# An MLP up projection by seven block products, with the sums of its weights built in device memory

## The chip, the cores and the metric

One core of a Trainium2 chip. The metric is the device time of one execution in microseconds; the time before is the median of 3 runs, 828.88 us (828.78 to 829.03). Engines: TensorE (PE, with its weight loads as PEld), VectorE (DVE), ScalarE (ACT), GpSimd (POOL), SyncE (SP, which here only issues DMAs).

## The reference

A transformer-like encoder layer on 512 tokens of width 1024, in float32: a recurrent mixer, cross-attention to 256 memory tokens, a squared-ReLU MLP with 4096 hidden units, a final norm. What the change touches is the last step of the layer:

```python
def squared_relu_mlp(xn, w_up, w_down):
    return jnp.square(jax.nn.relu(xn @ w_up)) @ w_down
...
x = x + squared_relu_mlp(rmsnorm(x, norm_mlp[l]), w_up[l], w_down[l])
return rmsnorm(x, norm_final)
```

`rmsnorm` divides each token's row by its root mean square and multiplies by a gain per column.

## The kernel before

**Precision.** Every float32 product is made of three reduced-precision ones. An operand is split into a high part (a ScalarE copy) and the remainder (a VectorE subtraction); `split_out` (L258) does both. `mm3` (L261 to L263) then issues high x high, high x remainder, remainder x high into one sum in PSUM. The program's order on TensorE is that of the code from the output projection on (`manual_schedule`); on the other engines a scheduler decides it, helped by `high_priority` and by orderings written by hand (`behind`).

**Weights.** They lie in device memory as blocks of 128x1024 (512 KB) in the order in which they are used. `load` (L236) brings a block into one of three staging buffers (`st`) through SP's queue; `split` makes its two parts in one of three pairs (`wh`, `wl`). `weights` splits two blocks ahead and loads one more.

**Seven products.** A product of 2x2 blocks can be made with seven block products in place of eight, when sums of blocks of both operands are used. The output projection of the attention (`by_blocks(-1)`) and the down projection (`by_blocks(f)`) work so: seven products P1 to P7, each in two column groups, makes 14 jobs of 12 matmuls of 512 wide. The sums of weight blocks come from `sum_loads` and `add_block` (L1086 to L1102): GpSimd issues DMAs that load a block into SBUF and accumulate others on top. Products go into PSUM banks and are added into the residual x by VectorE (L1222 in the output projection, L1285 in the MLP).

**The MLP before.** After the output projection, `turn_two` (L1236 to L1243) transposes x into `x3T`, four transposes to a bank, with the gain applied and the two parts made straight from PSUM. The root mean square is not applied to x: `rms_row` (L1264 to L1268) puts its reciprocal (`r4`, a power on GpSimd, L1261) into a row over tokens, and the evacuation of the up product multiplies by it: `max(product, 0) * rrow` on VectorE (L1342), then a square on ScalarE (L1343). The hidden units are done in four passes f of 1024. In each, the up projection is made directly: eight weight blocks of 24 matmuls, each 512 tokens wide. Sums and differences of the hidden activations are made and split (L1350 to L1366), then the down projection follows with seven products. The first up projection starts while the last of x is still being added: `first_two` (L1305 to L1324) uses the finished half of x's columns first.

## Time and profile before

| | |
|---|---|
| median of 3 runs | 828.88 us |
| profiled execution | 828.9 us, its span 826.9 us |
| granted TensorE clock | 0.998 |
| matmuls from the first up product to the last down product | 1440 of 512 wide, starts 491.64 to 819.20 us |
| weight loads by SP | 131 of 512 KB |
| transfers by GpSimd into sums | 76 of 512 KB |

The profile is of one execution. A row of a timeline gives start, duration, engine, line, operation, output and inputs, shape and count, and in brackets the idle time before it and what ended that. A row of grouped lines gives busy time and mean ns of one, then the idle time before. A DMA share is that of the core's 16 DMA engines, averaged.

### The profile page before, as it was taken

The page shows a single profiled execution, that of the slowest core. Times are in us where ns is not written, and L with a number is a line of the kernel's source. Part 1 is how long each engine was busy: PE and PEld are TensorE (multiplying, and loading weights), DVE is VectorE, ACT ScalarE, POOL GpSimd, SP SyncE. Part 2 cuts the span into 40 slices and gives each one's busy share as a digit, 9 for nine tenths or more (in the row PEclk, how much of TensorE's full clock was granted, in tenths as well). Part 3 has the DMA queues.
Part 4 walks back from the last instruction along what each step waited for, and adds up shares of the span by engine and source line. Part 5 has one row for each costly group of instructions (what it writes and reads, how often), then busy time and mean ns, then how long its engine had stood idle before and what let it go on. Part 6 is the DMA issues. An engine that isn't in the chain of part 4 may idle for free.

```text
span 826.9 us, 12625 instructions
## 1 busy us (share of the span) xinstructions
PE 813.4 (98%) x4862; PEld 676.1 (82%) x4862; DVE 590.9 (71%) x1046; ACT 431.9 (52%) x771; POOL 77.7 (9%) x131
## 2 busy tenths in 40 slices
PE   8999999999999999999999999999999999999996
PEld 6788778877878988887888888888888888888885
DVE  6568975699479898545668985676668566756685
ACT  5247564545578485345455675443454345434544
POOL 2000000100010000100100004022102210211001
PEclk9999999999999999999999999999999999999999
DMA  7332223322342334532343349969836982798332
GB/s 277 118 120 91 78 79 106 100 89 79 102 128 78 128 128 154 151 98 83 111 119 76 81 128 302 254 171 275 217 102 182 280 211 91 189 290 207 110 70 101
DMA packets 34125, 118.91 MB, mean 144 GB/s; under 512 B 3921, under 2 KB 4049, under 8 KB 34066
## 3 DMA queue, kind: packets, MB, share of 16 engines
q1 hardware_dynamic: 22832, 77.80, 27.5%
q0 software_dynamic: 10944, 39.85, 21.8%
q8 instruction: 38, 0.62, 0.3%
q10 hardware_dynamic: 290, 0.47, 0.1%
q14 instruction: 21, 0.17, 0.1%
HBM read 116.00 MB, written 2.10 MB: 143 GB/s over the span
## 4 chain that ended last, share of the span: by engine, by line
PE 84%; issue 6%; DVE 6%; ACT 2%; DMA 1%; POOL 1%; POOLq 0%; ACTq 0%; DVEq 0%
PE mm L261 17%; PE mm L263 17%; PE mm L262 17%; PE sm L1153 6%; PE sm L1155 6%; PE sm L1154 6%; PE mm L1153 2%; PE mm L1155 2%; PE mm L1154 2%; DVE wl L258 2%; PE sm L827 1%; PE sm L562 1%; PE sm L486 1%; ACT wh L258 1%; DVE t L759 1%
## 5 line engine op out<-in xcount | busy, mean ns | idle before, releaser
L258 ACT ACTIVATE wh<-st 128x1024 fp32r<-128x1024 f32 x131 | 138.7, 1060 | 185.2 <-PE mm L262 117.9
L261 PE MATMUL mm<-xT,wh 128*128 128x512 f32 x544 | 215.3, 396 | 0.0
L258 DVE TENSOR_TENSOR wl<-st,wh 128x1024 fp32r<-128x1024 f32 x131 | 160.1, 1223 | 76.1 <-ACT wh L258 75.6
L263 PE MATMUL mm<-xT,wl 128*128 128x512 f32 x544 | 212.8, 391 | 0.1
L262 PE MATMUL mm<-xT,wh 128*128 128x512 f32 x544 | 212.4, 390 | 0.3 <-DVE xT L975 0.3
L263 PEld LDWEIGHTS mm<-xT,wl 128*128 128x128 f32 x544 | 102.1, 188 | 21.9 <-DVE wl L258 0.3
L262 PEld LDWEIGHTS mm<-xT,wh 128*128 128x128 f32 x544 | 102.3, 188 | 20.8 <-DVE xT L975 0.9
L261 PEld LDWEIGHTS mm<-xT,wh 128*128 128x128 f32 x544 | 102.2, 188 | 20.7 <-ACT wh L258 0.3
L1102 POOL DMA_DIRECT2D as<-in_wpk x52 | 39.6, 763 | 250.2 <-DVE wl L258 162.0
L1342 DVE SCALAR_TENSOR_TENSOR t<-mm,rg 128x512 f32<-128x512 f32 x32 | 22.0, 691 | 52.1 <-PE mm L263 52.0
L1153 PE MATMUL sm<-wh,yT 128*128 128x512 f32 x128 | 49.8, 389 | 0.0
L1154 PE MATMUL sm<-wl,yT 128*128 128x512 f32 x128 | 49.8, 389 | 0.0
L1155 PE MATMUL sm<-wh,yT 128*128 128x512 f32 x128 | 49.8, 389 | 0.0
L258 ACT ACTIVATE wh<-as 128x1024 fp32r<-128x1024 f32 x26 | 27.6, 1062 | 37.0 <-PE sm L1155 23.7
L258 DVE TENSOR_TENSOR wl<-as,wh 128x1024 fp32r<-128x1024 f32 x26 | 31.9, 1226 | 14.0 <-ACT wh L258 14.0
L1153 PE MATMUL sm<-wh,a 128*128 128x512 f32 x84 | 32.9, 391 | 0.0
L1155 PE MATMUL sm<-wh,a 128*128 128x512 f32 x84 | 32.7, 389 | 0.0
L1154 PE MATMUL sm<-wl,a 128*128 128x512 f32 x84 | 32.7, 389 | 0.0
L1285 DVE TENSOR_TENSOR vv<-vv,sm 128x512 f32<-128x512 f32 x48 | 31.0, 681 | 1.7 <-PE sm L1155 1.7
L199 POOL TENSOR_TENSOR tiny<-tiny,misc 128x4 f32<-128x4 f32 (+1 forms) x10 | 9.6, 963 | 201.3 <-DVE tiny L197 136.2
L1155 PEld LDWEIGHTS sm<-wh,yT 128*128 128x128 f32 x128 | 24.0, 188 | 5.0
L1154 PEld LDWEIGHTS sm<-wl,yT 128*128 128x128 f32 x128 | 24.0, 188 | 5.0
(329 smaller groups left out, 1566.8 us busy)
## 6 DMA issues: line engine op xcount, KB each, us to landing
st<-in_wpk SPq DMA_DIRECT2D x131, 512.0 KB, 3.4
as<-in_wpk POOLq DMA_DIRECT2D x52, 512.0 KB, 6.9
gate<-in_wpk POOLq DMA_DIRECT2D x24, 512.0 KB, 7.1
as<-in_x SPq DMA_DIRECT2D x4, 512.0 KB, 6.8
vv<-in_x SPq DMA_DIRECT2D x8, 256.0 KB, 4.0
out<-vv SPq DMA_DIRECT2D x7, 256.0 KB, 2.2
a<-in_mem SPq DMA_DIRECT2D x2, 512.0 KB, 3.7
t<-in_rows SPq DMA_DIRECT2D x2, 256.0 KB, 5.3
```

The lines of the kernel that those rows point to most:

```text
L199: gp.tensor_tensor(out=r, in0=ms, in1=nh.to_broadcast([P, w]), op=ALU.pow)
L258: return sc.activation(dst_hi, src, AF.Copy), v.tensor_tensor(out=dst_lo, in0=src, in1=dst_hi.bitcast(F32), op=ALU.subtract)
L261: pe.matmul(ps, lhsT=ah, rhs=bh, start=first, stop=False)
L262: pe.matmul(ps, lhsT=ah, rhs=bl, start=False, stop=False)
L263: pe.matmul(ps, lhsT=al, rhs=bh, start=False, stop=last)
L486: mm = pe.matmul(ps[b * i:b * i + b, z:z + b], lhsT=kc[j][:, w * P + b * i:w * P + b * i + b], rhs=rhs(j, w * P, i), start=True, stop=True)
L1102: return gp.dma_start(out=dst, in_=wpk[idx], **kw)
L1153: pe.matmul(ps, lhsT=ah, rhs=bh, start=new, stop=False, **fl)
L1154: pe.matmul(ps, lhsT=ah, rhs=bl, start=False, stop=False, **fl)
L1155: pe.matmul(ps, lhsT=al, rhs=bh, start=False, stop=end and k == 1, **fl)
L1285: added = v.tensor_tensor(out=z, in0=z, in1=ps, op=ALU.add if sign > 0 else ALU.subtract)
L1342: v.scalar_tensor_tensor(out=y, in0=ps, scalar=0.0, in1=rrow[:, 0:512], op0=ALU.max, op1=ALU.mult)
```

## The change

The up projection of each pass is now made by seven block products too (`up`): the tokens are halved into 256 and 256, the 1024 columns of x into two halves, the hidden units into two. A stage has 14 products (P1 to P7, groups a and b of hidden units) of 24 matmuls, 128x256 each. `MORDER` sets the order of products by hand; in all up stages but the first, group a is mostly ahead of group b. Stages are numbered 0 to 7, even ones up, odd ones down.

Sums of weight blocks for the up products P4 to P7, and for P7 of the down product, are built in device memory. `make_forms` yields the steps: a copy of a block into a form (or of one form into another) on SP, and an accumulating DMA on GpSimd. `next_form` issues one step per weight block that an earlier part of the program uses, and on every second product in the MLP. In all there are 40 copies and 40 accumulations, of which 9 and 15 are left when the MLP begins. The finished forms are loaded like plain blocks. The sums for P5, P6, P4 of the down product stay in SBUF, in two buffers (`msum`) filled by `sum_base` on SP and `sum_add` on GpSimd.

As the products are added and subtracted before the ReLU, the root mean square must be applied to x before them. It is done in two halves of tokens: `rstd_half` makes the power of a half, `flip` transposes, ScalarE evacuates with the gain (L1396), `norm_half` transposes the reciprocals, puts them into a row (L1430), multiplies x by it (`times_r`, L1417) and makes and splits the sums of x that the products need (L1439 to L1445). The evacuation of the up product is then ReLU and square on ScalarE, with sums on VectorE around them. Splits per pass rise from 22 to 28.

The diff, cut to its core:

```diff
+    def next_form():
+        o = next(form_steps, None)
+        if o is not None:
+            behind(o, last_load[0] if o.ins.engine == mybir.EngineType.SP else last_made[0])
...
+        if i >= 6 and (i < 46 or i % 3):
+            next_form()
...
+    def mblock(st, g, kh, c):
+        f = st // 2
+        if st % 2:
+            return wpk[SIDX["t", "down", f * 8 + 2 * g + 4 * kh, 512 * c]]
+        i = SIDX["d", "up", 0, 1024 * f + 512 * c + 256 * g]
+        return wpk[i:i + 2, :, kh * 512:kh * 512 + 512].rearrange("n p c -> p n c")
+    def mfill(eng, dst, st, g, b, accumulate=False):
+        kw = dict(accum_op=ALU.add) if accumulate else {}
+        if st % 2 == 0:
+            dst = dst.rearrange("p (n c) -> p n c", n=2)
+        return eng.dma_start(out=dst, in_=mblock(st, g, *b), max_dma_last_dim=4096, **kw)
...
+    def make_forms():
+        def steps(st):
+            f, todo = {}, []
+            for g in range(2):
+                for p in ("P5", "P7", "P6", "P4") if st % 2 == 0 else ("P7",):
+                    f[p, g] = mforms[st, p, g] = hbm.tile([P, 1024], F32, tag=f"f{st}{p}{g}", name=f"form_{st}_{p}_{g}")
+            def start(p, g):
+                return mfill(nc.sync, f[p, g][:, :], st, g, (0, 1))
+            def follow(src, dst, g):
+                return nc.sync.dma_start(out=f[dst, g][:, :], in_=f[src, g][:, :], max_dma_last_dim=4096)
+            def add(p, g, b):
+                formed.add((st, p, g))
+                return mfill(gp, f[p, g][:, :], st, g, b, True)
+            first = ("P7", "P5") if st % 2 == 0 else ("P7",)
+            for p in first:
+                todo += [(start, p, g) for g in range(2)]
+            for p in first:
+                todo += [(add, p, g, (1, 1) if p == "P7" else (0, 0)) for g in range(2)]
+            if st % 2 == 0:
+                for src, dst, b in (("P7", "P6", (0, 0)), ("P6", "P4", (1, 0))):
+                    todo += [(follow, src, dst, g) for g in range(2)] + [(add, dst, g, b) for g in range(2)]
+            return todo
+        for s0 in (0, 4):
+            lanes = [steps(s0), steps(s0 + 1) + steps(s0 + 3), steps(s0 + 2)]
+            while any(lanes):
+                for w in lanes:
+                    if w:
+                        fn, *args = w.pop(0)
+                        yield fn(*args)
+    form_steps = make_forms()
...
+    MORDER = []
+    for q in range(4):
+        MORDER += [seq("1a 2a 1b 6a 5a 7a 3a 4a 5b 6b 2b 7b 3b 4b" if q else "1a 2a 1b 2b 5a 5b 3a 6a 6b 7a 7b 4a 3b 4b"),
+                   two(*("P1", "P5", "P6", "P2", "P7", "P3", "P4") if q < 3 else ("P1", "P5", "P2", "P6", "P3", "P7", "P4"))]
+    MJ = [(st, p, g) for st in range(8) for p, g in MORDER[st]]
...
+    def mload(n):
+        if n < len(MJ) and n not in mst:
+            st, p, g = MJ[n]
+            if st % 2 and p in ("P5", "P6", "P4"):
+                mst[n] = msum[p != "P5"][:, g * 1024:g * 1024 + 1024]
+                return
+            mst[n] = T("st", 1024, 3)
+            if p in PLAIN:
+                last_load[0] = mfill(nc.sync, mst[n][:, :], st, g, PLAIN[p])
+            else:
+                assert (st, p, g) in formed
+                last_load[0] = nc.sync.dma_start(out=mst[n], in_=mforms[st, p, g][:, :], max_dma_last_dim=4096)
...
+    def sum_base(st, p, g):
+        t = msum[p != "P5"][:, g * 1024:g * 1024 + 1024]
+        if p == "P5":
+            mfill(nc.sync, t, st, g, (0, 1))
+        else:
+            assert (st, "P7", g) in formed
+            nc.sync.dma_start(out=t, in_=mforms[st, "P7", g][:, :], max_dma_last_dim=4096)
+    def sum_add(st, p, g):
+        mfill(gp, msum[p != "P5"][:, g * 1024:g * 1024 + 1024], st, g, (1, 0) if p == "P4" else (0, 0), True)
...
+            mload(n)
+            hi, lo = T("wh", 1024, 3, F32R), T("wl", 1024, 3, F32R)
+            last_made[0] = split_out(hi, lo, mst[n])[1]
+            mhl[n] = (hi, lo)
+            if st % 2 and p == "P6":
+                due.append((n + 1, sum_add, st, "P4", g))
+            if st % 2 and p in ("P5", "P4") and st < 7:
+                q = {"P5": "P5", "P4": "P6"}[p]
+                due.append((n + 3, sum_base, st + 2, q, g))
+                due.append((n + 7, sum_add, st + 2, q, g))
+        return mhl[n]
...
+    def mahead(n):
+        with tc.high_priority():
+            for m in range(n, n + 3):
+                msplit(m)
+            for m in range(n + 3, n + 7):
+                mload(m)
+        if n % 2:
+            next_form()
+        return mhl[n]
...
+        with (tc.high_priority() if (t, c) in ((1, 1), (3, 0)) else ExitStack()):
             stats(st2, t, c)
+            if (t, c) in ((1, 1), (3, 0)):
+                rstd_half(t // 2)
+        if (t, c) == (2, 0):
+            turn_x2[0] = [smb(), smb()]
+            later.append([1, lambda: flip(turn_x2[0], (2,), 0)])
+        elif (t, c) == (3, 0):
+            later.append([0, lambda: flip(turn_x2[0], (3,), 0)])
+            later.append([1, lambda: norm_half(1)])
+        elif t % 2:
+            later.append([0 if (t, c) == (1, 1) else 3, lambda: flip([smb(), smb()], (t - 1, t), c)])
+            if (t, c) == (1, 1):
+                later.append([1, lambda: norm_half(0)])
...
+    def flip(banks, ts, c):
+        for i, ps in enumerate(banks):
             for k in range(2):
...
+                for t in ts:
+                    z = k * 256 + (t % 2) * P
+                    pe.transpose(ps[:, z:z + P], xr[t, c][:, (2 * i + k) * P:(2 * i + k) * P + P], ident)
+        t = ts[-1]
+        if t % 2 == 0:
+            return
...
+                sc.activation(fx[t // 2, c][:, kk * 256:kk * 256 + 256], banks[kk // 2][:, (kk % 2) * 256:(kk % 2) * 256 + 256], AF.Copy,
+                              scale=vc[:, V_MLP + 4 * c + kk:V_MLP + 4 * c + kk + 1])
+            if (t, c) == (3, 0):
+                sraw[0] = A4()
+                for h in range(2):
+                    z = slice(h * 512, h * 512 + 512)
+                    v.tensor_tensor(out=sraw[0][:, z], in0=fx[1, 0][:, z], in1=fx[1, 1][:, z], op=ALU.subtract)
...
+    def times_r(x, u, h):
+        z = x[:, h * 512:h * 512 + 512]
+        r = rrow[:, u * 256:u * 256 + 256]
+        v.tensor_tensor(out=z.rearrange("p (k t) -> p k t", t=256), in0=z.rearrange("p (k t) -> p k t", t=256),
+                        in1=r.unsqueeze(1).to_broadcast([P, 2, 256]), op=ALU.mult)
+    def part_split(p, x, h):
+        z = slice(h * 512, h * 512 + 512)
+        split_out(xf[p][0][:, z], xf[p][1][:, z], x[:, z])
+    def norm_half(u):
+        ps = smb()
+        for t in range(2):
+            pe.transpose(ps[:, t * P:t * P + P], rt[u][:, t:t + 1].to_broadcast([P, P]), ident)
+        with tc.high_priority():
+            sc.activation(rrow[:, u * 256:u * 256 + 256], ps[:, 0:256], AF.Copy)
+            for p, x in ((("P1", fx[0, 0]), ("P2", fx[0, 1])) if u == 0 else (("P5", sraw[0]),)):
+                for h in range(2):
+                    times_r(x, u, h)
+                    part_split(p, x, h)
+        if u == 0:
+            return
+        d = sraw[0]
+        x1, x3_, x2_, x4 = fx[0, 0], fx[0, 1], fx[1, 0], fx[1, 1]
+        v.tensor_tensor(out=d, in0=d, in1=x1, op=ALU.subtract)
+        v.tensor_tensor(out=x3_, in0=x3_, in1=d, op=ALU.add)
+        split_out(*xf["P3"], x3_)
+        split_out(*xf["P6"], d)
+        for h in range(2):
+            times_r(x2_, 1, h)
+        v.tensor_tensor(out=x1, in0=x1, in1=x2_, op=ALU.subtract)
+        split_out(*xf["P7"], x1)
+        for h in range(2):
+            times_r(x4, 1, h)
+        split_out(*xf["P4"], x4)
...
+        def square(t, src):
+            sc.activation(t, src, AF.Relu)
+            sc.activation(t, t, AF.Square)
+        def form(p, g, src, buf):
+            t = buf(F32R)
+            split_out(t[:, 0:512], t[:, 512:1024], src)
+            forms[p, g] = t
...
+        for n, (p, g) in enumerate(MORDER[st]):
+            hi, lo = mahead(len(JOBS) * st + n)
...
+            ps = B[g] if p == "P2" else C[g] if p in ("P5", "P3") else A[g]
+            xh, xl = xf[p]
+            for k in range(2):
+                o = ps[:, k * 256:k * 256 + 256]
+                for kt in range(4):
+                    z = slice(k * 512 + kt * P, k * 512 + kt * P + P)
+                    m = slice(kt * 256, kt * 256 + 256)
...
+                    pe.matmul(o, lhsT=hi[:, z], rhs=xh[:, m], start=new, stop=False, **fl)
+                    pe.matmul(o, lhsT=hi[:, z], rhs=xl[:, m], start=False, stop=False, **fl)
+                    pe.matmul(o, lhsT=lo[:, z], rhs=xh[:, m], start=False, stop=kt == 3, **fl)
+                after_product()
+            if p == "P1":
+                y[0, g] = msum[g][:, 2048:2560]
+                sc.activation(y[0, g], ps, AF.Copy)
+            elif p == "P2":
+                v.tensor_tensor(out=y[0, g], in0=y[0, g], in1=ps, op=ALU.add)
+                square(y[0, g], y[0, g])
+                form("P1", g, y[0, g], yt)
+            elif p == "P5":
+                y[3, g] = T2()[:, 0:512]
+                sc.activation(y[3, g], ps, AF.Copy)
+            elif p == "P6":
+                y[1, g] = rrow[:, (1 - g) * 512:(1 - g) * 512 + 512]
+                sc.activation(y[1, g], ps, AF.Copy)
+            if p in ("P3", "P6") and {("P3", g), ("P6", g)} <= set(MORDER[st][:n + 1]):
+                z = y[1, g]
+                v.tensor_tensor(out=z, in0=C[g], in1=z, op=ALU.subtract)
+                square(z, z)
+                form("P2", g, z, G4)
+            if p == "P7":
+                with tc.high_priority():
+                    v.tensor_tensor(out=y[3, g], in0=y[3, g], in1=ps, op=ALU.subtract)
+                square(y[3, g], y[3, g])
+                form("P4", g, y[3, g], A4)
+            elif p == "P4":
+                y[2, g] = T2()[:, 0:512]
+                square(y[2, g], ps)
+                first(g)
...
-        o = sum_loads(f, ("T2", "U", "T3") if f == 0 else ("T2",))
-        if f == 0:
-            for a in o:
-                behind(a, r4_made)
...
-                    ps, = proj_d("up", 1024 * f + P * (p + 4 * j), x3, count=1)
-                y = T2()[:, 0:512]
-                v.scalar_tensor_tensor(out=y, in0=ps, scalar=0.0, in1=rrow[:, 0:512], op0=ALU.max, op1=ALU.mult)
-                sc.activation(y, y, AF.Square)
...
+        sta, ready = up(2 * f)
...
+        by_blocks(2 * f + 1, sta, (sm2, mm2, sm2), lambda t, c, ps, sign, last: add_to(t, c, ps, sign, f == 3 and last), ready)
```

VectorE's order at the hand-over from the output projection to the up projection, before. `vv` is the residual x, `mm` and `sm` PSUM banks, `st` a staged weight block, `wh` and `wl` its parts, `xT` the transposed x, `tiny` and `misc` statistics.

```order
L1222 TENSOR_TENSOR vv_3545<-vv_3545,mm_4531 128x512
L258 TENSOR_TENSOR wl_5027<-st_4831,wh_5026 128x1024
L979 TENSOR_TENSOR tiny_4969<-misc 128x4
L981 TENSOR_SCALAR tiny_4971<-tiny_4969 128x4
L1243 SCALAR_TENSOR_TENSOR xT_4526<-sm_5008,vc,xT_4526 128x256
L1243 SCALAR_TENSOR_TENSOR xT_4526<-sm_5017,vc,xT_4526 128x256
...
L258 TENSOR_TENSOR wl_5097<-st_4913,wh_5096 128x1024
L258 TENSOR_TENSOR wl_5101<-st_4919,wh_5100 128x1024
L1342 SCALAR_TENSOR_TENSOR t_786_5072<-mm_4994,rg_4975 128x512
```

And now; `a_751` and `a_782` hold x's transposed halves for P1 and P2, `rg` the row of reciprocals.

```order
L1363 TENSOR_TENSOR vv_3630<-vv_3630,mm_4635 128x512
L1417 TENSOR_TENSOR a_751_4903<-a_751_4903,rg_4634 128x512 x2
L1417 TENSOR_TENSOR a_782_5044<-a_782_5044,rg_4634 128x512
L325 TENSOR_TENSOR xT_4624<-a_751_4903,xT_4624 128x512
L325 TENSOR_TENSOR wl_5023<-st_4931,wh_5022 128x1024
L325 TENSOR_TENSOR wl_5112<-st_4957,wh_5111 128x1024
...
L325 TENSOR_TENSOR xT_4624<-a_782_5044,xT_4624 128x512
...
L1363 TENSOR_TENSOR vv_3632<-vv_3632,mm_4636 128x512
...
L1409 TENSOR_TENSOR tiny_5095<-misc 128x2
L1410 TENSOR_SCALAR tiny_5096<-tiny_5095 128x2
```

Before, the last addition into x (vv_3545) came ahead of the weights' remainders and the statistics right behind. Now the last addition (vv_3632) stands behind two remainders of weights and the multiplications and splits of P1's and P2's x, and the second half's statistics behind it.

TensorE's order at the same place, before: the transposes with vv_3545, the second up block, and the transposes of the reciprocals.

```order
L1236 MATMUL sm_5017<-cs,vv_3545 128x128
L261 MATMUL mm_4995<-xT_4527,wh_4915 128x512
L262 MATMUL mm_4995<-xT_4527,wh_4915 128x512
L263 MATMUL mm_4995<-xT_4527,wl_4916 128x512
...
L1267 MATMUL sm_5066<-cs,tiny_4973 128x128 x4
L261 MATMUL mm_5106<-xT_4526,wh_5026 128x512
```

And now: P1a in `sm_5117`, the transposes of the last of x in its middle, those of the second half's reciprocals behind it, then P2a in `mm_5187`.

```order
L1553 MATMUL sm_5117<-xT_4624,wl_5017 128x256
L1389 MATMUL sm_5074<-cs,vv_3632 128x128 x2
L1389 MATMUL sm_5075<-cs,vv_3632 128x128 x2
L1551 MATMUL sm_5117<-xT_4624,wh_5016 128x256
L1552 MATMUL sm_5117<-xT_4624,wh_5016 128x256
...
L1428 MATMUL sm_5154<-cs,tiny_5099 128x128 x2
L1551 MATMUL mm_5187<-xT_4624,wh_5022 128x256
```

The reciprocals' transposes, once behind four groups of 12 wide matmuls of the first up blocks, now stand behind the 24 narrow ones of P1a alone.

GpSimd's order now, from the second power on (`form` is a tile in device memory, `as` one of the two sum buffers).

```order
L1412 TENSOR_TENSOR tiny_5099<-tiny_5096,misc 128x2
L282 DMA form_P_1_3344<-in_wpk 256x1x512
L282 DMA form_P_0_3327<-in_wpk 256x1x512
L282 DMA form_P_0_3337<-in_wpk 128x1024
L282 DMA form_P_0_3339<-in_wpk 256x1x512
L282 DMA form_P_1_3331<-in_wpk 256x1x512
L282 DMA form_P_1_3338<-in_wpk 128x1024
L282 DMA form_P_1_3343<-in_wpk 256x1x512
L282 DMA as_5101<-in_wpk 128x1024
```

Seven accumulations into forms stand right behind that power; before, the sums in SBUF for the first down projection stood behind the one power there was.

More of the change, by code (lines that the diff above doesn't have):

```diff
@@ L1125, in job @@
                     behind(a, b)
[L1126 to L1128 removed]
+            jobs_hl[n] = (hi, lo)
+            if p == "P7":
+                add_block(s_, block(-1, g, 0, 0))
             if p == "P6":
[L1130 to L1131 removed]
+                add_block(s_, block(-1, g, 1, 0))
+        return jobs_hl[n]
+    two = lambda *ps: [(p, g) for p in ps for g in range(2)]
@@ L1144, in by_blocks @@
+    def by_blocks(st, sta, banks, done, ready=None, after=None):
+        mlp = st >= 0
+        user = {"P1": 0, "P2": 1, "P5": 2, "P6": 0, "P3": 2, "P7": 0 if mlp else 3, "P4": 0}
+        opens = {"P1", "P2", "P5"} if mlp else {"P1", "P2", "P5", "P7"}
+        jobs = MORDER[st] if mlp else JOBS
         held = {}
@@ L1218, in heads_in, with after_product @@
             drain()
+    later = []
+    def after_product():
+        for w in list(later):
+            w[0] -= 1
+            if w[0] < 0:
+                later.remove(w)
+                w[1]()
+    fx, rt, sraw = {}, {}, [None]
     def add_out(t, c, ps, sign, last):
         z = xr[t, c]
-        last_add[0] = v.tensor_tensor(out=z, in0=z, in1=ps, op=ALU.add if sign > 0 else ALU.subtract)
-        if last:
+        v.tensor_tensor(out=z, in0=z, in1=ps, op=ALU.add if sign > 0 else ALU.subtract)
+        if not last:
+            return
+        with (tc.high_priority() if (t, c) in ((1, 1), (3, 0)) else ExitStack()):
```

261 lines of the change are left out of this document (124 added, 137 removed).

## The prediction

> **What bounds the kernel now.** I read the page first, then the stretches of the MLP, then TensorE's timeline at a few places, then the DMA by stretch. The page's line of busy time:
>
> ```profile
> PE 813.4 (98%) x4862; PEld 676.1 (82%) x4862; DVE 590.9 (71%) x1046; ACT 431.9 (52%) x771; POOL 77.7 (9%) x131
> ```
>
> The stretches (us, then busy time of PE, PEld, DVE, ACT, POOL, then TensorE's granted clock, the DMA share, GB/s). The first two lie ahead of the MLP, 472:508 is the hand-over from the output projection to the first up projection, the next two are MLP passes 0 and 2, the last is pass 3 with the tail:
>
> ```profile
> 299.00:383.00 84.00, 84.00 (x440) 70.09 (x440) 56.17 (x128) 48.27 (x123) 3.50 (x4) 1.00 0.40 126
> 384.00:472.00 88.00, 87.74 (x446) 73.89 (x445) 61.76 (x120) 47.16 (x94) 6.30 (x8) 1.00 0.36 95
> 472.00:508.00 36.00, 36.00 (x179) 30.08 (x178) 26.40 (x42) 22.35 (x43) 9.43 (x13) 1.00 0.65 195
> 508.00:587.00 79.00, 79.00 (x350) 65.44 (x349) 54.13 (x76) 36.31 (x47) 13.72 (x18) 1.00 0.91 240
> 665.00:743.00 78.00, 78.00 (x345) 64.59 (x345) 52.93 (x73) 34.60 (x43) 11.13 (x15) 1.00 0.71 191
> 743.00:827.00 84.00, 76.58 (x338) 63.06 (x337) 57.83 (x89) 41.52 (x63) 6.98 (x9) 0.98 0.46 126
> ```
>
> TensorE fills the whole of every MLP stretch at a granted clock of 1.00, and nothing else does; only the DMA engines come near it, at 0.91 in pass 0. So time goes with TensorE's work, as long as nothing takes its place. What one matmul costs is read from the distance of starts, since ends are modelled (TensorE's timeline; start, duration, engine, line):
>
> ```profile
> 394.29 0.28 PE L261 MATMUL sm<-a,yT 128*128 128x256 f32 x1
> ...
> 397.04 0.28 PE L263 MATMUL sm<-a,yT 128*128 128x256 f32 x1
> ...
> 491.64 0.39 PE L261 MATMUL mm<-xT,wh 128*128 128x512 f32 x1
> ...
> 494.13 0.39 PE L263 MATMUL mm<-xT,wl 128*128 128x512 f32 x1
> 494.36 1.03 PE L1236 MATMUL sm<-cs,vv 128*128 128x128 f32 x8
> 495.15 0.48 PE L261 MATMUL mm<-xT,wh 128*128 128x512 f32 x1
> ...
> 819.20 0.39 PE L1155 MATMUL sm<-wh,a 128*128 128x512 f32 x1
> ```
>
> Between the first pair lie 23 steps: 2.75/23 = 0.1196 us for a 256-wide matmul. Between the second pair lie 11: 2.49/11 = 0.2264; over longer runs it is 0.2267, which I take. The MLP starts at 491.64 and its last matmul at 819.20: 1440 x 0.2267 = 326.4 of those 327.6 us. 0.1196 is more than half of 0.2267: each matmul carries some 0.012 us that doesn't shrink with its width, in a stretch where TensorE waited for nothing.
>
> **Term 1, the products.** Per pass, before: 8 blocks x 24 = 192 matmuls of 512, 43.5 us. After: 14 products x 24 = 336 of 256, 40.2 us. That is 3.3 us per pass and 13.2 over four (seven eighths of the multiplications would be 21.8; the narrower form gives 8.6 back). Transposes and the down products keep their number. Bounds, from rounding in the two steps: 13.0 to 13.4.
>
> **Term 2, the hand-over into the first up stage.** Before, the rms factor is applied after the product (L1342), so the products need only transposed x. After, x is multiplied by it first, halved, summed into seven forms and split, on VectorE and ScalarE, and the first product can't start without it. Their rows (steps that follow each other at once show the true pace):
>
> ```profile
> 482.87 0.62 ACT L955 ACTIVATE t<-vv 128x512 f32<-128x512 f32 x1
> 483.39 0.19 ACT L955 ACTIVATION_READ_ACCUMULATOR t<-vv 128x1 f32 x1
> 483.65 0.91 ACT L1242 ACTIVATE xT<-sm,vc 128x256 fp32r<-128x256 f32 x2
> ...
> 489.80 0.82 ACT L1242 ACTIVATE xT<-sm,vc 128x256 fp32r<-128x256 f32 x2
> 490.51 1.06 ACT L258 ACTIVATE wh<-st 128x1024 fp32r<-128x1024 f32 x1
> ...
> 509.32 1.07 ACT L258 ACTIVATE wh<-st 128x1024 fp32r<-128x1024 f32 x1 [0.65 <-PE mm L262]
> 510.29 1.14 ACT L258 ACTIVATE yT<-t 128x512 fp32r<-128x512 f32 x2
> ```
> ```profile
> 546.00 1.23 DVE L258 TENSOR_TENSOR wl<-as,wh 128x1024 fp32r<-128x1024 f32 x1 [0.30 <-ACT wh L258]
> 547.14 1.28 DVE L1285 TENSOR_TENSOR vv<-vv,mm 128x512 f32<-128x512 f32 x2
> ```
> ```profile
> L1302 POOL TENSOR_TENSOR tiny<-tiny,misc 128x1 f32<-128x1 f32 x4 | 2.7, 666 | 26.6 <-DVE tiny L1299 26.6
> L1261 POOL TENSOR_TENSOR tiny<-tiny,misc 128x4 f32<-128x4 f32 x1 | 1.0, 1032 | 21.0 <-DVE tiny L981 21.0
> ```
>
> VectorE: 1.14 us per 1024 wide, 0.60 per 512 (0.68 until its result can be used). ScalarE: 0.97 per 1024, 0.55 per 512, 0.36 per 256, 0.75 for a row of statistics with its read-out. The 128x2 power lies between 0.67 and 1.03; I take 0.72.
>
> I walk the three engines' orders of the changed program with these, from the end of product P3 of the output projection as 0. TensorE, unhindered, has 24 matmuls of P4 and 22 transposes (0.1 each, from the eight above) ahead of it and would start P1a (product P1, group a) at 7.6 and P2a at 11.1. The first power is ready at 4.0; its transposes stand at 4.3, so that is met. The factor's row is in place at 5.9, and VectorE starts multiplying. P1a's first half is split at 8.4. Then VectorE has the remainders of two weight blocks in its queue (8.4 to 10.6), the rest of P1 and P2's forms, and only behind them the addition into vv_3632 (L1363), at 12.4, though its product was done at 7.4. That addition holds up three things in turn: the transposes that stand in the middle of P1a wait until 13.1 and the second half of P1a until 13.6; the statistics and the second power come at 15.2; its transposes, which stand ahead of P2a in TensorE's order, end at 15.45. P2a so starts at 15.45 in place of 11.1: **4.4 us of stall**. VectorE then works through ten splits of weights and of x and the sums of x until P3's remainder is ready at 31.0, where TensorE arrives at 29.9: **1.1 us** more. After that TensorE is behind VectorE for good: in the whole first up stage VectorE has 22 steps of 1.14 and 30 of 0.60, 43 us, against 40.2 of products, which is also why less than these 5.5 us is hard to get. Every hand-over of 0.05 us missed in the walk adds to it; bounds 4 to 7.
>
> In the other up stages VectorE has 14 x 1.14 + some 22 x 0.62 = 30 us and ScalarE 14 x 0.97 + 30 x 0.6 = 32, of 40; weights are split two products (5.7 us) ahead. I cost the six extra splits per pass at nothing there; without that lead each would cost up to 2.2 us.
>
> **Term 3, the transfers.** Pass 0 of before, then the first 24 us of its burst, then the quiet part of the program (queue: packets, MB, share of 16 engines; issues: count, size, us to landing):
>
> ```profile
> q0 software_dynamic: 3130, 11.39, 65.7%
> q1 hardware_dynamic: 2063, 7.53, 25.2%
> ...
> st<-in_wpk SPq DMA_DIRECT2D x13, 512.0 KB, 6.4
> ```
> ```profile
> q0 software_dynamic: 1367, 5.01, 76.2%
> q1 hardware_dynamic: 572, 2.09, 24.5%
> ...
> st<-in_wpk SPq DMA_DIRECT2D x4, 512.0 KB, 8.7
> ```
> ```profile
> st<-in_wpk SPq DMA_DIRECT2D x78, 512.0 KB, 3.3
> ```
>
> q1 is SP's, q0 GpSimd's accumulating transfers. 7.53 MB are 14.4 blocks of 0.524 MB: 0.252 x 79/14.4 = 1.38 us of all 16 engines for a load; 11.39 MB are 21.7, 0.657 x 79/21.7 = 2.39 us for a sum. The change adds 40 copies on SP and 40 sums on GpSimd into device memory. Ahead of the MLP, 31 of the copies and 25 of the sums are spread over some 450 us: 31 x 1.38 + 25 x 2.39 = 102.5 us, which lifts the share from about 0.4 to 0.6: free. Left over for the MLP are 9 copies and 15 sums. Pass 0 then has 31 SP transfers and 14 sums: 42.8 + 33.5 = 76.3 us in 78.3 us of products; pass 1 30 and 13: 72.5; passes 2 and 3 some 51. Before, pass 0 had 0.91 x 79 = 71.9 without one wait of TensorE. What differs is the pace: a job now takes 24 x 0.1196 = 2.87 us in place of 5.4, so a load is due twice as often, and seven of the sums stand on GpSimd right behind the second power, so they all start in the first up stage. Three staging buffers let a load land 9.5 us after its buffer came free before TensorE waits; under the burst it took 8.7. SP's queue also holds each form copy behind the sum it reads (a wait on GpSimd's transfer), with the loads queued behind it. No row shows a sum whose target is device memory; I bound it by the 2.39 of one into SBUF and by twice that (one more pass through memory), and take the lower. I put the term at 2 us; bounds 0 (all hidden, like before) and 4 in the forecast; more is a rival.
>
> **Sum.** Against the profiled execution, 828.9 us (span 826.9 and 2.0 around it; the median of the runs shown is 828.88, so no correction): 828.9 - 13.2 + 5.5 + 2 = **823.2 us**. The tail behind the last matmul (7.7 us of the span) is unchanged. Bounds: 828.9 - 13.4 + 4 + 0 = 819.5 and 828.9 - 13.0 + 7 + 4 = 826.9.
>
> **Rivals.**
> 1. No stall at the hand-over and none by transfers: 828.9 - 13.2 = 815.7. For it: VectorE has 9 us of slack in 472:508. Against it: its order is fixed, and the addition stands behind the splits. 0.11.
> 2. A 256-wide matmul costs half a 512-wide one in these stages: 4 x (43.5 - 336 x 0.1133) = 21.8; 828.9 - 21.8 + 5.5 + 2 = 814.6. Against it stand the 24 rows at 0.1196. 0.04. The Trainium skill (TensorE: Matmul & The Clock Gate, "Back-to-back issue gap") gives 262 cycles at a width of 256 and 518 at 512, nearly the half; by it the saving would be an estimated 19 us and the time 817. The trace does not agree: 0.1196 against 0.1092 by the page.
> 3. Transfers become the bound in passes 0 and 1, which makes it slower. When GpSimd's queue is never empty and SP's gets half of the engines, a load takes 2.76 us: 31 x 2.76 = 85.6 in pass 0 against 78.3 (+7.3), 30 x 2.76 = 82.8 in pass 1 (+4.5). In place of term 3 that is 828.9 - 13.2 + 5.5 + 11.8 = 833.0. It decides from a load that lands more than 9.5 us after its buffer came free. For it: the 24.5% that SP had under the burst, and 8.7 us to landing; sums into device memory at the double price would add 8 x 2.39 = 19 us of transfers in pass 0 alone. Against it: 0.91 in pass 0 without a wait. 0.17. The Trainium skill (DMA: Bandwidth & Descriptors, "Queues, rings and completion order") says that a DMA engine takes turns between queue rows packet by packet; that speaks for the half rather than for a quarter. No row here shows two queues that are both full.
> 4. Between the forecast and rival 3, with 5 to 8 us lost to transfers: 827.2 to 830.5, about no change. 0.08.
>
> **Chances.** Forecast 0.60, rivals 0.11, 0.04, 0.17, 0.08. A measurement of this kernel can tell about 0.2% from no change: 827.2 to 830.5. Faster: 0.60 + 0.11 + 0.04 = 0.75; same 0.08; slower 0.17. The range, 815 to 832, takes in the forecast with its bounds, rivals 1 and 4 and the low end of rival 3; it leaves out rival 2 and most of 3.
>
> **What would show it.** Right: starts of up matmuls 0.1196 apart; one gap or several of together 4 to 7 us in TensorE's row between the first up product and the second, put down to VectorE's addition at L1363 or to L1428; one of about 1 us at P3a; no wait of TensorE for splits in passes 2 and 3; DMA share near 0.95 in pass 0. Wrong: up matmuls faster than 0.115; no gap at P2a; ScalarE's splits waiting for loads in pass 0 or 1 and TensorE behind them; or waits at the border of up and down stages, where I found 1.2 us of slack.

## The result, and the profile after

The changed kernel takes 855.57 us (median of 4 runs, 854.45 to 860.29) against 828.85 before: ratio 1.0333, 95% interval 1.0294 to 1.0372. The forecast was 823.2, range 815 to 832. The profiled execution took 855.1 us, its span is 853.2.

The page's busy times, granted clock and DMA queues after:

```profile
PE 812.7 (95%) x5438; PEld 700.4 (82%) x5438; DVE 620.8 (73%) x1033; ACT 487.3 (57%) x854; POOL 92.7 (11%) x132
...
PEclk9999999999999999999999988999999999999998
...
q1 hardware_dynamic: 40624, 123.94, 41.7%
q0 software_dynamic: 15040, 39.85, 25.4%
```

TensorE's row was filled all but 13.5 us of the span before; now 40.5 are empty, and the granted clock has a dent in the middle. The stretches (us, PE, PEld, DVE, ACT, POOL, clock, DMA share, GB/s): the end of the output projection, the hand-over, then up and down stages in turn.

```profile
486.00:503.00 17.00, 9.92 (x48) 7.97 (x46) 7.09 (x12) 9.12 (x20) 0.71 (x1) 0.80 0.42 107
503.00:510.00 7.00, 4.48 (x33) 3.83 (x33) 6.41 (x11) 4.83 (x11) 1.23 (x2) 1.00 0.49 150
510.00:559.00 49.00, 41.25 (x313) 40.55 (x312) 37.13 (x42) 32.40 (x47) 6.51 (x7) 0.90 0.80 215
559.00:598.00 39.00, 38.08 (x167) 30.93 (x166) 32.51 (x42) 19.46 (x24) 4.79 (x6) 1.00 0.93 275
598.00:644.00 46.00, 43.38 (x336) 43.09 (x335) 29.67 (x34) 29.54 (x42) 6.89 (x7) 0.93 0.94 267
...
764.00:805.00 41.00, 40.60 (x337) 40.22 (x336) 29.65 (x34) 29.65 (x42) 0.00 (x0) 1.00 0.69 208
```

The last up stage runs as forecast; the first is 9 us too long, the second 6, and 17 us at the end of the output projection hold 9.9 in which TensorE is busy, part of them at a lower clock. TensorE's longest waits (in total, how many, the longest):

```profile
PE sm L1389 <- DVE vv L1363: 7.9, 2, 7.0
PE sm L1551 <- ACT rg L1567: 6.6, 4, 3.0
PE mm L1551 <- ACT t L1564: 3.6, 1, 3.6
```

The first is the wait of the last transposes of x, ahead of P1a. VectorE's addition is only the last link. The chain of waits there (start, us, what):

```profile
468.38 0.33 SPq L1223
468.71 0.05 issue
468.76 9.25 DMA as<-form_P
...
478.57 0.51 POOL as L282
479.08 13.08 DMA gate<-in_wpk
...
492.27 1.06 ACT wh L325
```

`gate` holds the weight sum of the output projection's last product P4. Its accumulation stands on GpSimd's queue behind the sums (`as`) of the first down stage, whose base comes from a form on SP's queue. Those eight transfers (four bases on SP, four accumulations on GpSimd), for products some 80 us later, fill the DMA engines; the one that is needed at once is issued 5.6 us later than before (479.08 against 473.53) and lands after 13.1 in place of 5.3. TensorE's row is empty for 7.1 us, and with the slow matmuls behind the gap P1a starts 9.4 us later than it could.

The third wait, and 3.0 us of the second, lie in the first up stage (2.6 more of the second in the second up stage). The third is that of product P3a, whose PSUM bank P5a's evacuation must free. GpSimd's timeline there, then ScalarE's (in brackets the idle time and what ended it):

```profile
508.77 0.69 POOL L1412 TENSOR_TENSOR tiny<-tiny,misc 128x2 f32<-128x2 f32 x1 [10.79 <-DVE tiny L1410]
509.42 5.20 POOL L282 DMA_DIRECT2D form_P<-in_wpk  x5
```
```profile
522.73 1.06 ACT L325 ACTIVATE wh<-st 128x1024 fp32r<-128x1024 f32 x1 [5.52 <-DMA st<-in_wpk]
525.36 1.06 ACT L325 ACTIVATE wh<-st 128x1024 fp32r<-128x1024 f32 x1 [1.57 <-DMA st<-form_P]
526.32 1.04 ACT L325 ACTIVATE yT<-a 128x1024 fp32r<-128x1024 f32 x1
527.26 0.58 ACT L1564 ACTIVATE t<-mm 128x512 f32<-128x512 f32 x1
...
530.72 1.06 ACT L325 ACTIVATE wh<-st 128x1024 fp32r<-128x1024 f32 x1 [1.93 <-DMA st<-form_P]
```

Right behind the second power five accumulations into forms are issued within 3 us. ScalarE then stands at splits whose blocks haven't landed (5.52 and 1.57 us), and the evacuation (L1564) that P3a waits for stands behind them. The 3.0 us of the second wait come later, at P7b, and are there without any forms, too (e1 below). DMA of that stage (510 to 559):

```profile
q0 software_dynamic: 1648, 3.67, 41.5%
q1 hardware_dynamic: 2128, 6.82, 38.5%
...
form_P<-in_wpk POOLq DMA_DIRECT2D x7, 512.0 KB, 12.5
st<-form_P SPq DMA_DIRECT2D x7, 512.0 KB, 8.3
```

A form accumulation takes 0.415 x 49/7 = 2.9 us of all engines. One into SBUF takes hardly less: between 566 and 580 us, where GpSimd's queue moved four of them and nothing else, 0.804 x 14/4 = 2.8. From 516 to 527, with the DMA engines full and both queues at work:

```profile
q0 software_dynamic: 600, 1.40, 66.8%
q1 hardware_dynamic: 555, 1.59, 40.2%
```

Packets and bytes went about evenly; time didn't, as GpSimd's packets take longer. SP so moved a block of 0.524 MB every 3.6 us (11 x 0.524/1.59). The Trainium skill (DMA: Bandwidth & Descriptors, "Queues, rings and completion order") says that an engine takes turns between queue rows, packet by packet. The trace agrees: 600 packets against 555.

Last, what each stall leaves behind. Four stretches in which the clock was halved:

```profile
492.20:499.00 6.80, 3.64 (x12) 3.06 (x13) 3.80 (x6) 5.79 (x14) 0.71 (x1) 0.50 0.14 28
526.30:533.10 6.80, 4.04 (x17) 3.75 (x18) 5.71 (x6) 4.87 (x7) 1.90 (x2) 0.50 1.08 312
546.80:550.20 3.40, 3.40 (x19) 3.40 (x18) 0.69 (x1) 0.79 (x2) 0.00 (x0) 0.50 0.35 135
615.10:621.80 6.70, 6.17 (x29) 6.17 (x30) 3.02 (x3) 2.88 (x4) 0.00 (x0) 0.50 1.08 298
```
```profile
530.66 0.41 PE L1553 MATMUL mm<-yT,wl 128*128 128x256 f32 x1
530.87 0.41 PE L1551 MATMUL mm<-yT,wh 128*128 128x256 f32 x1
...
533.53 0.28 PE L1553 MATMUL mm<-yT,wl 128*128 128x256 f32 x1
533.65 0.28 PE L1551 MATMUL mm<-yT,wh 128*128 128x256 f32 x1
```

Each begins within or just behind a gap of TensorE, of 7.1, 3.7, 3.2 and 2.8 us, and lasts 3.4 or 6.8 us; matmuls are 0.21 us apart in it in place of 0.12. Added up over the slow matmuls that is some 7 us. The Trainium skill (TensorE: Matmul & The Clock Gate, "HAM oscillation — how this bites in real kernels") warns of idle gaps beyond some 3.4 us. The trace agrees for the two longer ones; here gaps of 3.2 and 2.8 us were followed by a halved clock, too.

What P1a waits for at the hand-over, in the changed kernel and, last, in e4 (below), where the addition into x comes early:

```profile
PE sm L1552 <- DVE xT L325: 1.0, 1, 1.0
PE sm L1389 <- DVE vv L1363: 0.9, 1, 0.9
PE sm L1551 <- ACT xT L325: 0.6, 1, 0.6
...
PE sm L1553 <- DVE xT L325: 1.7, 1, 1.7
```

Two remainders of weights (2.35 us on VectorE from 502.77) hold up a split of P1's own x first, and the addition into x behind it.

### The profile page after: what moved, and what is told of

It reads as the page before. It is cut to its first block, busy times and chain, and to the rows that moved or that the text cites. A ratio compares the mean times of both kernels' runs of the same rounds, so it can differ in the third digit from the quotient of the medians.

```text
span 853.2 us, 14086 instructions
## 1 busy us (share of the span) xinstructions
PE 812.7 (95%) x5438; PEld 700.4 (82%) x5438; DVE 620.8 (73%) x1033; ACT 487.3 (57%) x854; POOL 92.7 (11%) x132
## 3 DMA queue, kind: packets, MB, share of 16 engines
q0 software_dynamic: 15040, 39.85, 25.4%
## 4 chain that ended last, share of the span: by engine, by line
PE 55%; DVE 13%; DMA 12%; issue 9%; ACT 8%; POOL 1%; POOLq 0%; ACTq 0%; SPq 0%; DVEq 0%
PE mm L328 9%; PE mm L330 9%; PE mm L329 9%; DMA st<-in_wpk 6%; DVE wl L325 6%; ACT wh L325 5%; PE sm L1281 3%; PE sm L1280 3%; PE sm L1279 3%; DMA st<-form_P 3%; PE sm L1551 2%; PE sm L1552 2%; PE sm L1553 2%; DMA gate<-in_wpk 2%; PE mm L1552 1%
## 5 line engine op out<-in xcount | busy, mean ns | idle before, releaser
L325 DVE TENSOR_TENSOR wl<-st,wh 128x1024 fp32r<-128x1024 f32 x163 | 199.0, 1223 | 109.5 <-ACT wh L325 108.1
L328 PE MATMUL mm<-xT,wh 128*128 128x512 f32 x288 | 115.5, 402 | 0.0
L330 PE MATMUL mm<-xT,wl 128*128 128x512 f32 x288 | 113.1, 393 | 0.1
L329 PE MATMUL mm<-xT,wh 128*128 128x512 f32 x288 | 112.7, 391 | 0.3 <-DVE xT L1042 0.3
L1279 PE MATMUL sm<-wh,a 128*128 128x512 f32 x180 | 70.3, 390 | 1.2 <-DVE vv L1482 1.2
L1281 PE MATMUL sm<-wh,a 128*128 128x512 f32 x180 | 70.3, 391 | 0.9 <-DVE a L325 0.9
L330 PEld LDWEIGHTS mm<-xT,wl 128*128 128x128 f32 x288 | 54.1, 188 | 11.7 <-DVE wl L325 0.3
L329 PEld LDWEIGHTS mm<-xT,wh 128*128 128x128 f32 x288 | 54.2, 188 | 10.9 <-DVE xT L1042 0.9
L328 PEld LDWEIGHTS mm<-xT,wh 128*128 128x128 f32 x288 | 54.1, 188 | 10.8 <-ACT wh L325 0.3
L282 POOL DMA_DIRECT2D form_P<-in_wpk x40 | 42.7, 1508 | 68.9 <-DMA form_P<-form_P 53.1
L1551 PE MATMUL sm<-yT,wh 128*128 128x256 f32 x128 | 38.5, 301 | 6.6 <-ACT rg L1567 6.6
L1281 PEld LDWEIGHTS sm<-wh,a 128*128 128x128 f32 x180 | 33.8, 188 | 8.6 <-DVE a L325 1.6
L1279 PEld LDWEIGHTS sm<-wh,a 128*128 128x128 f32 x180 | 33.8, 188 | 8.5 <-ACT wh L325 1.6
L1552 PE MATMUL sm<-yT,wh 128*128 128x256 f32 x128 | 38.0, 297 | 0.0
L1553 PE MATMUL sm<-yT,wl 128*128 128x256 f32 x128 | 37.9, 296 | 0.0
```

The source lines that it names most:

```text
L282: return eng.dma_start(out=dst, in_=mblock(st, g, *b), max_dma_last_dim=4096, **kw)
L325: return sc.activation(dst_hi, src, AF.Copy), v.tensor_tensor(out=dst_lo, in0=src, in1=dst_hi.bitcast(F32), op=ALU.subtract)
L328: pe.matmul(ps, lhsT=ah, rhs=bh, start=first, stop=False)
L329: pe.matmul(ps, lhsT=ah, rhs=bl, start=False, stop=False)
L330: pe.matmul(ps, lhsT=al, rhs=bh, start=False, stop=last)
L1279: pe.matmul(ps, lhsT=ah, rhs=bh, start=new, stop=False, **fl)
```

## Experiments

Below, a run's loss is what its profiled span has beyond 813.2 us, an estimate of the span without stalls: 484.5 up to the end of P3 (e1, e9 and e12 come within 0.3 of it), 7.6 for P4 with its transposes, 313.7 for the MLP at 0.2267 and 0.1196 us a matmul, 7.4 for the tail. The stretches run from start to start on TensorE's timeline; those of the main runs:

| loss, us | changed | e1 | e13 | e2 | e3 | e10 |
|---|---|---|---|---|---|---|
| up to the end of P3 of the output projection | 1.4 | 0.1 | -0.2 | 1.1 | 4.7 | 0.6 |
| its P4 (24 matmuls, 22 transposes) | 9.4 | 8.8 | 8.7 | 0.2 | 10.4 | 0.2 |
| start of P1a to start of P2a | 3.4 | 3.4 | 3.4 | 5.0 | 4.6 | 4.4 |
| rest of the first up stage | 11.9 | 6.1 | 6.1 | 16.0 | 6.1 | 9.5 |
| first down stage | 1.5 | 1.5 | 1.4 | 1.5 | 1.5 | 7.8 |
| second up stage | 5.7 | 0.1 | 0.1 | 5.0 | 0.1 | 6.6 |
| the rest | 6.7 | 3.4 | 4.0 | 4.4 | 3.0 | 4.0 |
| sum | 40.0 | 23.4 | 23.5 | 33.2 | 30.4 | 33.1 |

The runs of one such kernel scatter by up to 0.8% (the kernel before by 0.1 to 0.3%), so medians a few us apart are told by the stretch that changed, too. The stretches are of the one execution that was profiled, which lies up to 5.5 us from the median (e5).

**e1, no forms.**

```diff
     def next_form():
-        o = next(form_steps, None)
...
+        return
...
-                last_load[0] = nc.sync.dma_start(out=mst[n], in_=mforms[st, p, g][:, :], max_dma_last_dim=4096)
+                last_load[0] = mfill(nc.sync, mst[n][:, :], st, g, (0, 1))
```

> The changed kernel without any form: the 40 copies and 40 accumulations into device memory are left out, and a plain weight block is loaded (or used as the base of a sum) wherever a form was, so the products P4 to P7 of the up stages and P7 of the down stages use wrong weights. All products, splits and loads into SBUF stay as many as they were. Theory A (the loss comes from transfers: sums ahead of others on GpSimd's queue before the MLP, the burst of form accumulations in the first up stage, and the lower granted clock behind each stall): 822 to 830 us; what stays is the hand-over on VectorE (3 to 4) and the four early sums of the first down stage. Theory B (the loss comes from the narrower products themselves, whose splits and evacuations ScalarE and VectorE can't keep up with): 848 us or more.

842.78 us, ratio 1.0171 [1.0154, 1.0188]: between the two. By the medians the forms cost 13 us (16.6 by the profiled executions), and three things stay that aren't theirs. TensorE's waits from 470 us on:

```profile
PE sm L1385 <- DVE vv L1359: 7.4, 2, 6.5
PE sm L1547 <- ACT rg L1563: 3.8, 3, 3.0
PE sm L1275 <- DVE vv L1478: 1.1, 1, 1.1
PE sm L1548 <- DVE xT L323: 1.0, 1, 1.0
PE mm L1548 <- DVE yT L323: 1.0, 1, 1.0
```

The gap ahead of the last transposes is still there (its sums don't need forms), and so is the wait for an evacuation on ScalarE (product P6, group b), with no load late any more. From the second up stage on nearly nothing is lost: theory B, that splits can't keep up with narrow products, falls there.

**e13, copies without accumulations.**

```diff
             def add(p, g, b):
                 formed.add((st, p, g))
-                return mfill(gp, f[p, g][:, :], st, g, b, True)
+                return None
```

> The changed kernel with the 40 accumulations into device memory left out and their 40 copies kept (so the forms are copies of single blocks, wrong as weights). Theory A (GpSimd's accumulations are what delays the loads): as without any form, 838 to 845 us. Theory J (the copies on SP's queue delay the loads behind them just as much): 849 or more.

839.61 us, 1.0123 [1.0100, 1.0145], stretch by stretch as e1. The 40 copies on SP cost nothing; GpSimd's accumulations cost it all, 16 us by the medians. In principle SP's queue could also have stood still behind forms that weren't finished; in the two up stages of the changed kernel its waits are for staging buffers and loads, none for an accumulation. In e13 loads landed in 3.9 and 3.6 us in the first up stage:

```profile
st<-form_P SPq DMA_DIRECT2D x7, 512.0 KB, 3.9
st<-in_wpk SPq DMA_DIRECT2D x6, 512.0 KB, 3.6
```

**e2, the first sums behind the second power.**

```diff
-                fn(1, q, g)
+                behind(fn(1, q, g), rt_made[1])
```

> The changed kernel with one thing moved: the four bases and four accumulations of the first down stage's sums are ordered behind the second power, in place of the last 25 us of the output projection. Theory A: the 7 us gap ahead of the output projection's last transposes goes, with the low clock behind it, about 8 us; the four accumulations join the burst in the first up stage, which gives 0 to 6 back: 847 to 855 us. Theory B: 855, no change. Theory C (what counts is the total of the transfers, not their place): 855, no change.

850.38 us, 1.0266 [1.0234, 1.0298]. The 9.4 us of P4 fall to 0.2; 4.1 come back in the first up stage and 1.6 in P1a, where the sums joined the burst. The move so gains 5 us, not 9.

**b1, the same mechanism in the kernel before.**

```diff
-        if f == 0:
-            for a in o:
-                behind(a, r4_made)
```

> The kernel before with one line of order left out: the accumulations of the first MLP pass's sums no longer have to stand behind the power on GpSimd, so that eleven of them come ahead of the output projection's last accumulations on GpSimd's queue. TensorE's and SP's orders stay as they are. Theory A (sums that are needed later, placed ahead of one that is needed now, hold TensorE up by their transfers): a gap of 7 us or more ahead of product P4 of the output projection, 836 to 846 us. Theory G (it takes the device memory forms to cause the gap): 829, no change.

835.15 us, 1.0071 [1.0056, 1.0086]: 6 us from the order of one queue, less than the bound that was given. TensorE's gap is 2.8 us in place of the 7 expected; with it the clock is halved for 6.8 us. GpSimd's timeline: the last accumulation that the output projection needs (`gate`) now comes at 476.64 in place of 473.53, behind seven others.

```profile
476.09 0.86 POOL L1102 DMA_DIRECT2D as<-in_wpk  x1 [4.57 <-DMA as<-in_wpk]
476.64 1.22 POOL L1102 DMA_DIRECT2D gate<-in_wpk  x1
479.92 2.65 POOL L1102 DMA_DIRECT2D as<-in_wpk  x3 [2.06 <-DMA as<-in_wpk]
```

Forms aren't needed for this gap (theory G falls).

**e3, all form steps ahead of the output projection.**

```diff
-        if i >= 6 and (i < 46 or i % 3):
+        if i >= 6:
             next_form()
+            if 20 <= i < 44:
+                next_form()
```

> The changed kernel with all 80 form steps issued ahead of the output projection (two steps per weight block in a middle part of the program), so that none is left for the MLP; their number and bytes are the same. Theory A: the first up stage loses its burst (some 9 of the 12 us that it takes too long) and the second up stage its own (some 4 to 5 of 5.7); the gap in the output projection stays: 838 to 845 us. Theory C (total of the transfers): 851 to 856, for the bytes are the same. Theory B: 855.

846.53 us, 1.0215 [1.0199, 1.0231], 1.5 above theory A's range. The same bytes, and both up stages lose just what they lose without forms (6.1 and 0.1): place counts, not the total (theory C falls). But 3.3 us come back early, where the denser steps make loads late ahead of the recurrent chunks.

**e10, the form steps one by one.** e8 below, with 24 steps left for the MLP and each accumulation behind its copy.

> As e8, but with the form steps at the pace of the changed kernel, so that 24 of them are left for the MLP, and each accumulation ordered right behind its copy, so that SP's queue hands them out one by one and no burst of seven can start. Theory H (it is the burst that hurts, not the amount in the stage): the first up stage loses 2 to 5 us and the whole is within 3 us of e8. Theory C' (what counts is the amount in a stage: 21 SP transfers of 1.5 us, four sums of 2.4 and six form accumulations of 3.3 are 61 us, in a stage of 42): the first up stage and the next together lose 12 us or more, 838 us or more.

849.27 us, 1.0241 [1.0224, 1.0258], 12 us above e8: no burst of more than three, and yet the rest of the first up stage loses 9.5 us (e8: 1.5) and the second 6.6 (e8: 0.8). Within one stage it is the amount that hurts; taking the burst apart doesn't help. Theory H falls. DMA from 499 to 552 us, in 40 slices:

```profile
DMA  5001825899998999999999999999999999999999
...
st<-form_P SPq DMA_DIRECT2D x7, 512.0 KB, 8.3
st<-in_wpk SPq DMA_DIRECT2D x6, 512.0 KB, 9.1
```

**e4, the last addition into x early.** In `add_out` the addition into vv_3632 is given `high_priority`, which puts it ahead of two weight remainders.

> The changed kernel with VectorE's last addition into x (vv_3632) placed ahead of the two remainders of weight blocks that stood before it, nothing else. Theory A, by the walk of the prediction: the transposes in the middle of P1a and the second power come 2 to 3 us earlier, but the burst of accumulations behind that power then comes earlier too, and the loads set the end of the stage: 852 to 855 us. Theory D (the hand-over on VectorE is a large part of the loss and what comes behind follows from it): 846 or less.

855.58 us, no change (P1a 2.8 for 3.4, and 0.8 more behind it). Theory D falls. So the addition's place is worth 0.6 us; the two weight remainders stay in the way, and P1a waits for its own x behind them.

**e5, e6, e7, mends together.** e5 is e2 and e3; e6 adds `high_priority` for P6's evacuation (L1567); e7 adds e4.

> Both moves together: the first down stage's sums behind the second power, and all form steps ahead of the output projection. Work of TensorE alone is 815.7 us. Theory A (the losses are separate places and add up): 4.7 from the denser form steps in the early part, 0 in the output projection, 4 to 5 in P1a, 6 to 9 in the rest of the first up stage, 1.5 in the first down stage, 3 in the rest: 833 to 840 us. Theory C (total of the transfers): 844 or more.

> The run before plus one thing: ScalarE's evacuation of product P6, on which product P7 of the same group waits for its PSUM bank, is placed ahead of the ReLUs and squares that stood before it. Theory E (the gap of 3 us ahead of P7b in the first up stage, with the low clock behind it, is only this place in ScalarE's order): 3 to 5 us less than the run before. Theory F (ScalarE has no room in that stretch and the wait only moves on): within 1.5 us of it.

> The run before plus VectorE's addition into vv_3632 ahead of the two remainders of weight blocks. Theory A: the hand-over shortens by 1 to 3 us, now that no burst of form accumulations stands behind the second power: 827 to 833 us, at or just above the kernel before. Theory D (the hand-over causes what follows): below 826.

847.37 (1.0226 [1.0209, 1.0243]), 843.30 (1.0167 [1.0138, 1.0196]) and 841.40 us (1.0155 [1.0136, 1.0173]). The first and the last are above theory A's ranges; e5's 847.37 lies where theory C, the total of the transfers, put it, and only the stretches speak against C. In e5 the two moves don't add up: the sums behind the second power meet the loads there (rest of the first up stage 11.6, a wait of 4 us at P3a). e6 is 4 us below e5, as theory E had it: the evacuation takes 5.6 us out of that stage and puts 1.7 at the border to the down stage. e4's step gives 1 to 2 at most, which the intervals don't tell from nothing.

**e8 and e9, the sums spread out; e9 without forms.** Besides the edit shown, both have e6's and e4's edits; e8 issues all form steps ahead of the output projection, one per weight block and one more at every fourth, e9 none.

```diff
...
-                fn(1, q, g)
+        due.append((4 + 2 * i, lambda q=q, g=g: behind(sum_base(1, q, g), last_load[0])))
+        due.append((8 + 2 * i, lambda q=q, g=g: behind(sum_add(1, q, g), rt_made[1])))
```

> All mends together: the form steps ahead of the output projection but thinned out (one per weight block and one more at every fourth), the first down stage's sums issued one by one through the first up stage, each base behind a load on SP's queue, P6's evacuation and the addition into vv_3632 early. Theory A: 2 to 4 us lost in the early part, 0 in the output projection, 3 to 4 in P1a, 2 to 4 in the rest of the first up stage, 3 in the first down stage, 2 in the rest: 828 to 833 us, about the kernel before. Theory D (VectorE's and ScalarE's hand-over, not the transfers, is what remains): 838 or more.

> The run before with every form left out: plain weight blocks are loaded where forms were, so P4 to P7 of the up stages and P7 of the down stages have wrong weights; all products, splits and loads stay. It shows what the seven products give when the sums of weights cost nothing. Theory A: 815.7 and 3 to 4 in P1a, 2 to 3 in the first up stage, 2 to 3 in the first down stage, 1 to 2 in the rest: 824 to 828 us, below the kernel before. Theory D: as the run before within 2 us.

837.52 (1.0100 [1.0076, 1.0123]) and 833.82 us (1.0052 [1.0036, 1.0067]), each between what its two theories gave. Even with no form at all, and the first sums spread out, the seven products in this order don't beat the kernel before. e9 loses 5.4 us at P1a, 2.6 in the rest of the stage and 7.8 at the border behind it.

**e11 and e12, ScalarE or VectorE.** e11 puts P6's evacuation of e9 back; e12 replaces ReLU and square on ScalarE in the first stage:

```diff
         def square(t, src):
+            if st == 0 and src is t:
+                v.scalar_tensor_tensor(out=t, in0=src, scalar=0.0, in1=src, op0=ALU.max, op1=ALU.mult)
+                return
             sc.activation(t, src, AF.Relu)
```

> As e9 (no forms, wrong weights in their place, the first sums spread, the addition into vv_3632 early), with P6's evacuation back in its old place. Theory F (ScalarE has more work in the first up stage than time, so that moving one of its steps ahead only moves the wait to the border of the down stage): the 7.8 us of the first down stage fall to 1.5 and the rest of the first up stage rises from 2.6 to 6: 829 to 832 us. Theory E (the evacuation's place alone was wrong): 836 or more.

> As e11, with ReLU and square in the first up stage made by one VectorE operation (max with 0, times itself) in place of two on ScalarE, where their source lies in SBUF. Theory F: ScalarE sheds 6 x 1.1 us of the first up stage, VectorE takes 6 x 0.6; the gap ahead of P7b and those at the border shorten by 2 to 4 us: 826 to 829 us. Theory I (VectorE, at 43 of some 45 us in that stage, is the bound there, and more work on it costs): at or above e11.

836.02 (1.0077 [1.0050, 1.0104]) and 834.17 us (1.0064 [1.0047, 1.0081]), not told apart from each other. By their times theory F lost twice: e11's stands where E put it, and e12's is above F's range. By the stretches, in e11 the border falls from 7.8 to 1.5 and the stage rises from 2.6 to 8.2, so the wait moves on, as theory F has it; in e12 the stage falls to 2.6 and the border rises to 9.5. With ScalarE relieved, VectorE is nearly full from the first up stage to the border (e12, 498 to 538.5 and to 549), and ScalarE waits for loads:

```profile
498.00:538.50 40.50, 38.84 (x320) 38.23 (x319) 37.70 (x45) 25.17 (x35) 3.52 (x5) 1.00 0.83 244
538.50:549.00 10.50, 8.78 (x41) 7.00 (x40) 9.22 (x14) 8.00 (x12) 0.85 (x1) 1.00 0.66 228
...
ACT wh L323 <- DMA st<-in_wpk: 7.0, 4, 2.5
```

VectorE is busy 37.7 of 40.5 us and 9.2 of 10.5; ScalarE at 25.2 has room. These changes of order move the wait, none removes it. That VectorE's work in the first stage (theory I) is what is left is likely, but not shown: no run takes work off VectorE, and the loads that ScalarE waits for 7.0 us, beside the sums spread over that stage, are a rival that wasn't tried. No variant beat the kernel before.

## Why the prediction was wrong, step by step

- **Term 1, the products: right.** In e3, where the later up stages wait for nothing, they last 40.3 us against 40.2 forecast and 43.5 before; in the changed kernel's own last up stage the starts are 0.12 us apart (763.73, 763.84, 763.96). The 13.2 us are there. Rival 2 falls.
- **Term 2, the hand-over: half the size.** P2a's part was 4.4 and is 3.4 (e1), P3a's 1.1 is 1.2. The link was named wrongly in part: the addition accounts for 0.9 of those 3.4 as a wait and for 0.6 when it is moved (e4); the two weight remainders ahead of it hold up P1a's own x just as well. Without P4's gap ahead of it P1a loses 3.2 to 5.4 (e7, e9). Missed are 3.2 us at P7b for ScalarE's evacuation of P6, 1.5 in the down stage behind it, and a halved clock behind the stalls: 3.4 + 6.1 + 1.5 = 11.0 in e1 in place of 5.5. The step that failed is the walk, which followed VectorE's queue to P3a and stopped there, though the text's own sum (43 us of VectorE for 40.2) said that the backlog goes on.
- **Term 3, transfers: the step that decided.** It was put at 2 us and is some 25 in the profiled executions: 16.6 for the form accumulations (40.0 against 23.4 in e1; 13 to 16 by the medians of e1 and e13) and 8.6 for the first sums where they stand (8.8 in e1, 0.2 in e2). Of the latter e2 gained only 5, as moved sums cost something at their new place. The working failed in three places. "Ahead of the MLP ... free" looked at shares of 0.4 and 0.6 averaged over hundreds of us, and not at the queues there: eight transfers with a later use started ahead of one with an immediate use. The first up stage was costed over the whole pass (76.3 us of transfers in 78.3), while its seven accumulations fell into its first half. And the 2.39 us were no price of an accumulation: before, GpSimd's queue also carries plain bases (six of the fourteen transfers for the first pass), and accumulations alone take 2.8 to 3.0.
- **Rival 3: right place, wrong price.** Its point of decision, a load landing more than 9.5 us after its buffer came free, was met by two of three loads (10.3, 9.4 and 12.3 us from issue in the burst). So was the forecast's own sign of being wrong: ScalarE's splits wait for loads in passes 0 and 1, and TensorE behind them. Its 833.0 took SP's rate as halved over two passes, 2.76 us a load; in the burst it was 3.6, as packets alternate and GpSimd's take longer. The loss came as stalls in three places, 5.8 and 5.6 us in two up stages beyond e1, and one before the MLP.
- **Not in the prediction at all:** the clock. Its only trace before was the 0.98 of the tail. In these runs a stall of some 3 us or more cost TensorE more than its own length; some 7 us of the 40 are slow matmuls.
- The four mends of e8 leave 837.5 where the forecast wanted 823: 24.8 us of loss stay in its profiled execution (839.74 us), 13.5 of them in the hand-over, the first up stage and its border.

Open: what bounds the first up stage and its border when the forms are gone; why e3 and e8 lose some 5 us in the early part, which was read from the waits (late loads) and not tried; 1.4 us in the last down stage that every variant has, and 1.2 to 1.4 of tail in all that keep form accumulations, weren't looked into.

## What to carry to other kernels

Give a transfer a place by when its result is needed: on an in-order queue, one that is needed in 80 us must not stand ahead of one that is needed now, and an average share of the DMA engines says nothing about that. Budget transfers by the stage in which they start, not by the pass. And when fewer, smaller products are bought with more work on other engines, add up those engines' work in the busiest stage first: here TensorE won 3.3 us a pass, and around the first up stage 11.0 were lost again even without forms (e1).

## What was not expected of the hardware

- An accumulating transfer of 512 KB took 2.8 us of all DMA engines into SBUF and 2.9 to 3.0 into device memory: 2.9 in the first up stage, 3.0 by GpSimd's queue as a whole (25.4% of 853.2 us against 11.5% of 836.7 in e13, over 40 accumulations). A plain load took 1.4 in the kernel before. The 40 copies within device memory took no more than that (42.9% against 37.0% of 836.7 us on SP's queue, e13 against e1: 1.2 us each).
- With both queues at work the DMA engines moved as many packets for one as for the other (600 and 555 in 11 us), so the queue with the slower packets had more of the time (66.8% against 40.2%).
- TensorE's granted clock fell to 0.50 with gaps of 2.8 to 7.1 us, for 3.4 or 6.8 us at a time; matmuls of 256 were then 0.21 us apart.
